# A new opening for an encoder kernel: quarters of x, first weights over two DMA queues, products by pairs of K blocks

## The chip, the cores and the metric

One Trainium2 chip, of which the program uses one core. The metric is the device time of one execution in microseconds (us); each version is run several times and the median is given.

## The reference

The kernel computes two layers of an encoder on 256 tokens of width 1024, all in float32. Each layer is a half-step feed-forward block, a mixer with two attention branches, and a second feed-forward block. The change touches the first feed-forward block of the first layer only:

```python
def rms_norm(x, g):
    y = x * lax.rsqrt(jnp.mean(x * x, axis=-1, keepdims=True) + EPS)
    return y * g

def swiglu(x, w_gate, w_up, w_down):
    return (jax.nn.silu(x @ w_gate) * (x @ w_up)) @ w_down

for l in range(2):
    x = x + 0.5 * swiglu(rms_norm(x, ffn1_norm[l]), ffn1_w_gate[l], ffn1_w_up[l], ffn1_w_down[l])
    ...   # neighbourhood attention and sliding-window attention, gated, into w_out
    x = x + 0.5 * swiglu(rms_norm(x, ffn2_norm[l]), ffn2_w_gate[l], ffn2_w_up[l], ffn2_w_down[l])
```

## The kernel before

The 256 tokens are two tiles of 128 (`t` is 0 or 1), and the width of 1024 is eight K blocks of 128. A float32 product is made of three products of rounded parts: every operand is split into a high part, made on ScalarE (ACT) by a copy, and a low part, the remainder, made on VectorE (DVE) by a subtraction. The high and low parts of x are the tiles `xh0, xl0` (tile 0) and `xh1, xl1` (tile 1); those of a piece of weights are `wh` and `wl`. Three matmuls then add x-high by w-high, x-high by w-low and x-low by w-high in PSUM. The helper `split_to` issues the two instructions of a split, `load` starts a weight transfer of 512 KB (two K blocks by 512 columns) into one of four buffers `raw` and splits it.

x stands with tokens on the partitions, so `norm` turns it on TensorE (PE): four transposes into a PSUM tile `tp`, a product with the gains (`gain`) into `xg`, and the split of `xg`. The factor of the norm itself (`rs_y`, one number for each token) is applied later, when the gate is taken. It comes from `square`: two sums of squares a tile on ACT, two small operations on DVE, a power on GpSimd (POOL).

The feed-forward block goes through its 2816 hidden columns in eleven chunks. A chunk has 256 gate and 256 up columns, which give one PSUM tile `g` of 512 columns for each token tile. The tiles `g` come from the pool `ps_g`, which has two buffers. When the 24 matmuls of a tile are done, ACT makes `sg` (the silu of the gate half) and DVE makes `hh` (times the up half); both read `g`, so its buffer is free only when `hh` is done, and the third `g` of the program goes into the buffer of the first.

`opening` replaces the first chunk's matmuls at the start of the program, where nothing is loaded yet. It interleaves the transfers, the norm without its factor, the first splits, warm-up matmuls on a blank tile (`warmup`), and the 48 products of chunk 0; it also issues the splits of the four weight pieces of chunk 1 (`second`) and the four squares.

The order on each engine comes from two places. The order on PE is that of the code. The order on DVE, ACT, POOL and of the DMA issues is made by a scheduler from a model of times when the program is built, except where the code chains instructions: `linked` ties each instruction of `opening` to the one before it on its engine, until `chain.clear()`.

Of the kernel before, what the change touches and what calls it, by code (L numbers as in the profile page):

```python
# [11 lines left out]
F32 = mybir.dt.float32  # L12
# [9 lines left out]
P = 128  # L22
# [34 lines left out]
def hybrid_encoder(ctx, tc, x, w_gu1, w_d1, w_in, b_gate, qk_gain, rpb, sink, t5,  # L57
# [20 lines left out]

    def fetch(t, h):
        if (t, h) == (0, 0):  # L80
            nc.sync.dma_start(wide[:, :HEAD + 512], x[:P, :HEAD + 512])
        else:
            nc.sync.dma_start(xs[t][:, h * 512:(h + 1) * 512],
                              x[t * P:(t + 1) * P, HEAD + h * 512:HEAD + (h + 1) * 512])

    fetch(0, 0)

# [7 lines left out]
    warmed = nc.scalar.activation(warm, ident[:, :1], AF.Silu)  # L95
# [92 lines left out]

    ssq = [None] * T

    def norm(t, n, half, apart=False):
        if half == 0:
            xT[t] = [act.tile([P, KD, P], F32R, name=f"x{p}{t}", tag=f"x{p}{t}") for p in "hl"]
            ssq[t] = small.tile([P, 2], F32, name="ssq", tag="ssq")
        ks = slice(4 * half, 4 * half + 4)
        tp = ps_tp.tile([P, 4, P], F32, name="tp", tag="tp")
        for i in range(4):
            k = 4 * half + i
            nc.tensor.transpose(tp[:, i, :], xs[t][:, k * P:(k + 1) * P], ident)
        xg = act.tile([P, 4, P], F32, name="xg", tag="xg", bufs=2)  # L200
        if apart and half == 1:
            for i in range(4):
                linked("act", lambda: nc.scalar.activation(xg[:, i, :], tp[:, i, :], AF.Copy,
                                                           scale=gain[:, n, 4 + i:5 + i]))
        else:
            linked("dve", lambda: nc.vector.tensor_tensor(
                xg, tp, gain[:, n, ks].unsqueeze(2).to_broadcast([P, 4, P]), ALU.mult))
        split_to(*(x[:, ks, :] for x in xT[t]), xg)
        if not apart:
            square(t, half)  # L210

    def square(t, half, junk=None):
        if junk is None:
            junk = act.tile([P, 512], BF16, name="junk", tag="xg", bufs=2)
        linked("act", lambda: nc.scalar.activation(junk, xs[t][:, half * 512:(half + 1) * 512], AF.Square,
                                                   accum_out=ssq[t][:, half:half + 1]))
        if half == 1:
            v = small.tile([P, 1], F32, name="ms", tag="ms")
            nc.vector.tensor_tensor(v, ssq[t][:, :1], ssq[t][:, 1:], ALU.add)
            nc.vector.tensor_scalar(v, v, 1.0 / D, EPS, op0=ALU.mult, op1=ALU.add)  # L220
            rstd[t] = rsqrt(v, 1)

    def opening(w, l):
        def piece(i, c=0):
            return load(w[l, 2 * i * P:(2 * i + 2) * P, c * 512:(c + 1) * 512].rearrange("(k p) n -> p k n", p=P),
                        2, 512)

        ps = [ps_g.tile([P, 512], F32, name="g", tag="g") for _ in range(T)]

        def steps(t, i):  # L230
            wh, wl = pieces[i]
            xh, xl = xT[t]
            for a, b in ((xh, wh), (xl, wh), (xh, wl)):
                for k in (2 * i, 2 * i + 1):
                    nc.tensor.matmul(ps[t], a[:, k, :], b[:, k % 2, :], start=a is xh and b is wh and k == 0,
                                     stop=b is wl and k == KD - 1)
            tick(2)

        pieces = []
        chain["act"] = warmed  # L240
        warmup(5)
        norm(0, 0, 0, True)
        pieces.append(piece(0))
        warmup(5)
# [17 lines left out]
        second += [piece(i, 1) for i in range(1, KD // 2)]  # L262
# [565 lines left out]
```

## Time and profile before

| | us |
|---|---|
| runs of the kernel | 1091.14, 1092.18, 1093.49 (median 1092.18) |
| the profiled execution | 1091.39 |
| its span, first to last instruction | 1089.6 |
| PE busy in the span | 1077.2 (99%) |
| DVE, ACT, POOL busy | 855.7 (79%), 658.7 (60%), 117.5 (11%) |
| read from memory | 210.59 MB, 194 GB/s over the span |

The views of the profile give times from the start of the span. A row of the timeline has the start, the length, the engine, the line of the code and the operation, what it writes and reads, and how many instructions were merged into the row; in brackets at its end stands how long the engine was idle before and what released it. PEld is the loading of the stationary operand, which runs beside the matmuls and shows waits more exactly than PE does; SPq is the queue that issues the transfers.

### The profile page before, as it was taken

Reading aid. Unit: us, or ns where it says so; the run is one execution under the profiler, and the core shown is the slowest. Engines: PE = TensorE matmul, PEld = TensorE weight load, DVE = VectorE, ACT = ScalarE, POOL = GpSimd, SP = SyncE. Lnnn points to the kernel's source line nnn. Section 1 sums busy time; section 2 is a strip of 40 time slices with the busy share of each in tenths; the row PEclk is TensorE's granted clock in tenths of the full one; section 3 lists DMA queues with packets and bytes.
Section 4 is the critical chain, followed back from the end, with each engine's and each line's share of the span. In section 5 each row is a group of like instructions: output and inputs, shape, how many; then the busy total and the mean of one; then the engine's idle time right before and its main releaser. Section 6 shows DMA issues by size and latency. Waiting matters only on the chain.

```text
span 1089.6 us, 14660 instructions
## 1 busy us (share of the span) xinstructions
PE 1077.2 (99%) x5137; PEld 889.5 (82%) x5137; DVE 855.7 (79%) x1298; ACT 658.7 (60%) x1002; POOL 117.5 (11%) x118
## 2 busy tenths in 40 slices
PE   9999999999999999999999999999999999999998
PEld 7888878888888888888878888888888888888887
DVE  6887787889886778778777787788888767878785
ACT  6665654788764556565465565457877646656552
POOL 1400000243520000000000000003534000000000
PEclk9999999999999999999999999999999999999999
DMA  8876565755654676666657766557666555776661
GB/s 241 267 222 216 189 197 171 234 189 152 189 179 135 201 224 212 210 197 203 193 172 219 228 204 211 162 164 236 183 190 178 178 166 166 225 235 198 212 188 71
DMA packets 98827, 212.63 MB, mean 195 GB/s; under 512 B 7568, under 2 KB 13744, under 8 KB 98752
## 3 DMA queue, kind: packets, MB, share of 16 engines
q1 hardware_dynamic: 98560, 211.60, 62.1%
q8 instruction: 40, 0.66, 0.2%
q0 software_dynamic: 192, 0.08, 0.1%
q14 instruction: 35, 0.29, 0.1%
HBM read 210.59 MB, written 1.06 MB: 194 GB/s over the span
## 4 chain that ended last, share of the span: by engine, by line
PE 86%; DVE 8%; ACT 3%; issue 2%; DMA 2%; ACTq 0%; DVEq 0%
PE g L168 19%; PE g L170 19%; PE g L169 19%; PE acc L168 5%; PE acc L170 5%; PE acc L169 5%; DVE wl L183 3%; PE tp L317 2%; ACT wh L182 1%; PE tp L168 1%; PE tp L169 1%; PE tp L170 1%; PE pt L572 1%; DMA raw<-in_w_d 1%; PE sc L551 1%
## 5 line engine op out<-in xcount | busy, mean ns | idle before, releaser
L183 DVE TENSOR_TENSOR wl<-raw,wh 128x1024 fp32r<-128x1024 f32 (+1 forms) x340 | 407.8, 1216 | 68.8 <-ACT wh L182 67.5
L182 ACT ACTIVATE wh<-raw 128x1024 fp32r<-128x1024 f32 (+1 forms) x340 | 348.9, 1046 | 111.9 <-PE g L170 35.0
L168 PE MATMUL g<-wh,xh 128*128 128x512 f32 (+1 forms) x976 | 389.9, 399 | 0.0
L170 PE MATMUL g<-wh,xl 128*128 128x512 f32 (+1 forms) x976 | 379.0, 388 | 0.7 <-DVE xl L183 0.7
L169 PE MATMUL g<-wl,xh 128*128 128x512 f32 (+1 forms) x976 | 377.6, 387 | 0.4 <-DVE wl L183 0.4
L170 PEld LDWEIGHTS g<-wh,xl 128*128 128x128 f32 x976 | 183.4, 188 | 41.4 <-DVE xl L183 2.1
L169 PEld LDWEIGHTS g<-wl,xh 128*128 128x128 f32 x976 | 184.1, 189 | 32.0 <-DVE wl L183 0.8
L168 PEld LDWEIGHTS g<-wh,xh 128*128 128x128 f32 x976 | 183.6, 188 | 30.9 <-DVE hh L449 0.2
L447 ACT ACTIVATE sg<-g,rs_y 128x256 f32<-128x256 f32 x88 | 41.4, 471 | 117.1 <-PE g L170 116.8
L347 DVE TENSOR_TENSOR u<-raw 128x512 f32<-128x512 f32 x56 | 38.7, 691 | 61.9 <-DMA raw<-in_w_d 61.3
L168 PE MATMUL acc<-wh,hi 128*128 128x512 f32 x200 | 79.3, 396 | 0.0
L170 PE MATMUL acc<-wh,lo 128*128 128x512 f32 x200 | 78.0, 390 | 0.0
L169 PE MATMUL acc<-wl,hi 128*128 128x512 f32 x200 | 77.9, 390 | 0.0
L174 POOL TENSOR_TENSOR rs_y<-ms,mhalf 128x1 f32<-128x1 f32 x12 | 6.7, 556 | 660.3 <-DVE ms L220 651.9
L449 DVE SCALAR_TENSOR_TENSOR hh<-g,rs_y,sg 128x256 f32<-128x256 f32 x88 | 42.2, 480 | 38.8 <-ACT sg L447 38.7
L182 ACT ACTIVATE corner<-raw 128x512 fp32r<-128x512 f32 x28 | 17.6, 630 | 54.7 <-DMA raw<-in_w_d 38.4
L564 POOL TENSOR_TENSOR S<-S,sm 128x512 f32<-128x512 f32 x32 | 37.2, 1161 | 71.4 <-DVE sm L563 45.2
L170 PEld LDWEIGHTS acc<-wh,lo 128*128 128x128 f32 x200 | 37.6, 188 | 8.1
L169 PEld LDWEIGHTS acc<-wl,hi 128*128 128x128 f32 x200 | 37.6, 188 | 7.4
L168 PEld LDWEIGHTS acc<-wh,hi 128*128 128x128 f32 x200 | 37.6, 188 | 7.4
L557 ACT ACTIVATE S<-S,mx 128x256 f32<-128x256 f32 x64 | 32.0, 501 | 7.4 <-DVE mx L554 7.4
L317 PEld LDWEIGHTS tp<-ident,hh 128*128 128x128 f32 x176 | 24.2, 140 | 14.1 <-DVE hh L449 3.4
(190 smaller groups left out, 1477.3 us busy)
## 6 DMA issues: line engine op xcount, KB each, us to landing
raw<-in_w_gu SPq DMA_DIRECT2D x176, 512.0 KB, 4.4
raw<-in_w_d SPq DMA_DIRECT2D x100, 512.0 KB, 4.3
raw<-in_w_in SPq DMA_DIRECT2D x64, 512.0 KB, 4.3
raw<-in_w_out SPq DMA_DIRECT2D x16, 512.0 KB, 3.6
bb<-in_b_gate SPq DMA_DIRECT2D x16, 256.0 KB, 3.5
raw<-in_w_bsw SPq DMA_DIRECT2D x8, 512.0 KB, 4.0
raw<-in_w_bna SPq DMA_DIRECT2D x8, 512.0 KB, 3.5
raw<-in_w_d SPq DMA_DIRECT2D x12, 256.0 KB, 2.6
```

Source lines behind the costliest of these rows:

```text
L168: nc.tensor.matmul(ps, xh, wh, start=first, stop=False)
L169: nc.tensor.matmul(ps, xh, wl, start=False, stop=False)
L170: nc.tensor.matmul(ps, xl, wh, start=False, stop=last)
L182: linked("act", lambda: nc.scalar.activation(hi, src, AF.Copy))
L183: linked("dve", lambda: nc.vector.tensor_tensor(lo, src, hi.bitcast(F32), ALU.subtract))
L317: nc.tensor.transpose(tp[:, SLOT[t][i], :], hh[:, i * P:(i + 1) * P], ident)
L347: sub = lambda to, x, y: nc.vector.tensor_tensor(to, x, y, ALU.subtract)
L447: nc.scalar.activation(sg, ps[:, :FC], AF.Silu, scale=rstd[t])
L449: nc.vector.scalar_tensor_tensor(hh, ps[:, FC:], rstd[t], sg, op0=ALU.mult, op1=ALU.mult)
L551: nc.tensor.matmul(ps[:, t, :], qT[:, h, t * P:(t + 1) * P], k[:, kidx(h), :], start=i == 0, stop=i == 1)
L557: nc.scalar.activation(S_[:, t, :], S_[:, t, :], AF.Exp, bias=mx[:, t:t + 1], scale=-1.0, accum_out=sm[:, t:t + 1])
L564: nc.gpsimd.tensor_tensor(S_, S_, sm.unsqueeze(2).to_broadcast([P, T, S]), ALU.mult)
```

## The change

- The x transfers are cut: the first half of each tile's width arrives as two quarters, and the first transfer is 192 KB (with the gains) in place of 320 KB.
- The first weight piece is issued by ACT, as two transfers of one K block (256 KB) each, beside SP's transfers; it was one of 512 KB on SP. The order on SP becomes: quarters of both tiles, the second piece, second halves of x, the rest.
- Turning, gain, split and products of the first half of x go by two K blocks at a time for both tiles; the first weight piece is split by one K block. The second half of x keeps its four K blocks.
- The four squares stay behind the last split of the opening in the code, as before.
- The loading of the silu table follows ACT's two transfers.

The core of the diff (`turned`, `gained`, `xpart`, `wpart` are the transposes, the gain and the two halves of a split for the K blocks named, each chained on its engine; `go` issues the products; the second letter of "hl" is the weights' part):

```diff
     def fetch(t, h):
         if (t, h) == (0, 0):
-            nc.sync.dma_start(wide[:, :HEAD + 512], x[:P, :HEAD + 512])
+            nc.sync.dma_start(wide[:, :HEAD + 256], x[:P, :HEAD + 256])
         else:
-            nc.sync.dma_start(xs[t][:, h * 512:(h + 1) * 512],
-                              x[t * P:(t + 1) * P, HEAD + h * 512:HEAD + (h + 1) * 512])
+            c0, c1 = (0, 256, 512, D)[h:h + 2]
+            nc.sync.dma_start(xs[t][:, c0:c1], x[t * P:(t + 1) * P, HEAD + c0:HEAD + c1])
...
+        def fetched(i, apart=None):
+            raws[i] = ring.tile([P, 2, 512], F32, name="raw", tag="raw", bufs=RAW)
+            for ks in (slice(0, 1), slice(1, 2)) if apart else (slice(0, 2),):
+                (apart or nc.sync).dma_start(raws[i][:, ks, :], source(i)[:, ks, :])
...
+        A, B, ALL = (0, 1), (2, 3), (0, 1, 2, 3)
+        fetched(0, nc.scalar)
         fetch(1, 0)
-        norm(1, 0, 0, True)
-        pieces.append(piece(1))
         fetch(0, 1)
         fetch(1, 1)
-        warmup(3)
-        steps(0, 0)
-        norm(0, 0, 1, True)
-        steps(1, 0)
-        pieces.append(piece(2))
-        norm(1, 0, 1, True)
-        pieces.append(piece(3))
+        chain["act"] = nc.scalar.activation(warm, ident[:, :1], AF.Silu)
+        fetched(1)
+        warmup(4)
+        turned(0, 0, A)
+        gained(0, 0, A, "dve")
...
+        go(0, (0,), "hh", "hl")
+        go(0, (1,), "hh")
+        go(0, (0, 1), "lh")
+        turned(0, 0, B)
+        gained(0, 0, B, "act")
+        go(1, (0, 1), "hh")
+        go(0, (1,), "hl")
+        go(1, (0, 1), "hl", "lh")
+        turned(1, 0, B)
+        fetch(0, 2)
+        fetch(1, 2)
+        fetched(2)
+        fetched(3)
+        gained(1, 0, B, "dve")
...
+        go(0, B, "hh", "lh")
+        go(1, B, "hh", "lh")
+        turned(0, 1, ALL)
+        turned(1, 1, ALL)
+        go(0, B, "hl")
+        go(1, B, "hl")
+        gained(0, 1, ALL, "act")
+        gained(1, 1, ALL, "dve")
+        xpart(0, 1, ALL, "h")
+        xpart(1, 1, ALL, "h")
+        wpart(2, (0, 1), "h")
...
         square(0, 0, idle)
         square(0, 1, idle)
-        second = [piece(0, 1)]
+        second = [load(source(0, 1), 2, 512)]
...
-        for i in (1, 2, 3):
+        for ks in ((4, 5), (6, 7)):
             for t in range(T):
-                steps(t, i)
+                go(t, ks, "hh", "lh", "hl")
```

The order on the engines changes in the first fifty or so instructions of DVE and ACT and is the same behind them. Two places are shown; a name's number tells one buffer of the program from another, and the line numbers are those of the version shown.

First, ACT in the opening. Before, from its first split to the last split of the four weight pieces of chunk 0 (`wh_130`, `wh_154`, `wh_189`, `wh_207`):

```order
L182 ACTIVATE xh0_116<-xg_124 128x512
L182 ACTIVATE wh_130<-raw_128 128x1024
L182 ACTIVATE xh1_140<-xg_148 128x512
L182 ACTIVATE wh_154<-raw_152 128x1024
L203 ACTIVATE xg_174<-tp_169,x0_82 128x128 x4
L182 ACTIVATE xh0_116<-xg_174 128x512
L182 ACTIVATE wh_189<-raw_187 128x1024
L203 ACTIVATE xg_198<-tp_193,x0_82 128x128 x4
L182 ACTIVATE xh1_140<-xg_198 128x512
L182 ACTIVATE wh_207<-raw_205 128x1024
```

Now, from the split of the second piece (`wh_123`) to that of the fourth; `tp_198` is the second half of tile 0 turned, `xg_205` that of tile 1 with its gain, made on DVE:

```order
L252 ACTIVATE wh_123<-raw_121 128x1024
L252 ACTIVATE xh1_145<-xg_144 128x256
L243 ACTIVATE xg_199<-tp_198,x0_82 128x128 x4
L252 ACTIVATE xh0_131<-xg_199 128x512
L252 ACTIVATE xh1_145<-xg_205 128x512
L252 ACTIVATE wh_177<-raw_175 128x1024
L252 ACTIVATE wh_181<-raw_179 128x1024
```

The splits of the third and fourth piece moved behind the gain and both splits of the second half of x; before, each tile's half was followed by one piece.

Second, the change from chunk 0 to chunk 1. Here ACT before, with the squares (L215), the splits of chunk 1's pieces (`wh_220` to `wh_245`) and the two `sg` of chunk 0:

```order
L215 ACTIVATE idle_104,ssq_118<-x0_82 128x512 x2
L182 ACTIVATE wh_220<-raw_218 128x1024
L215 ACTIVATE idle_104,ssq_142<-x1_83 128x512
L447 ACTIVATE sg_285<-g_109,rs_y_216 128x256
L215 ACTIVATE idle_104,ssq_142<-x1_83 128x512
L182 ACTIVATE wh_233<-raw_231 128x1024
L182 ACTIVATE wh_239<-raw_237 128x1024
L182 ACTIVATE wh_245<-raw_243 128x1024
L447 ACTIVATE sg_289<-g_110,rs_y_229 128x256
```

And ACT now, where chunk 1's pieces are `wh_236` to `wh_261` and tile 0's gate is `sg_289`:

```order
L207 ACTIVATE idle_103,ssq_110<-x0_82 128x512 x2
L181 ACTIVATE wh_236<-raw_234 128x1024
L207 ACTIVATE idle_103,ssq_111<-x1_83 128x512 x2
L181 ACTIVATE wh_249<-raw_247 128x1024
L181 ACTIVATE wh_255<-raw_253 128x1024
L181 ACTIVATE wh_261<-raw_259 128x1024
L523 ACTIVATE sg_289<-g_108,rs_y_232 128x256
L181 ACTIVATE wh_369<-raw_367 128x1024
L523 ACTIVATE sg_293<-g_109,rs_y_245 128x256
```

Tile 0's `sg` moved from behind the first piece of chunk 1 and three squares to behind all four pieces and all four squares.

DVE at the same place before:

```order
L219 TENSOR_TENSOR ms_213<-ssq_118 128x1
L220 TENSOR_SCALAR ms_213<-ms_213 128x1
L183 TENSOR_TENSOR wl_221<-raw_218,wh_220 128x1024
L449 SCALAR_TENSOR_TENSOR hh_287<-g_109,rs_y_216,sg_285 128x256
L219 TENSOR_TENSOR ms_226<-ssq_142 128x1
L220 TENSOR_SCALAR ms_226<-ms_226 128x1
L183 TENSOR_TENSOR wl_234<-raw_231,wh_233 128x1024
L183 TENSOR_TENSOR wl_240<-raw_237,wh_239 128x1024
L107 SCALAR_TENSOR_TENSOR qkg_96<-qkg_96 128x2 x2
L183 TENSOR_TENSOR wl_246<-raw_243,wh_245 128x1024
L449 SCALAR_TENSOR_TENSOR hh_291<-g_110,rs_y_229,sg_289 128x256
```

And DVE now; `qkg` are two small products that need a transfer issued by POOL after the last square's `rs_y`:

```order
L182 TENSOR_TENSOR wl_237<-raw_234,wh_236 128x1024
L211 TENSOR_TENSOR ms_242<-ssq_111 128x1
L212 TENSOR_SCALAR ms_242<-ms_242 128x1
L182 TENSOR_TENSOR wl_250<-raw_247,wh_249 128x1024
L182 TENSOR_TENSOR wl_256<-raw_253,wh_255 128x1024
L106 SCALAR_TENSOR_TENSOR qkg_95<-qkg_95 128x2 x2
L182 TENSOR_TENSOR wl_262<-raw_259,wh_261 128x1024
L525 SCALAR_TENSOR_TENSOR hh_291<-g_108,rs_y_232,sg_289 128x256
L182 TENSOR_TENSOR wl_370<-raw_367,wh_369 128x1024
```

Tile 0's `hh` moved from behind the first low part of chunk 1 (`wl_221`) to behind the fourth (`wl_262`) and behind `qkg`.

PE at this place now, with the waits; `g_297` is the first tile of chunk 1, the third of the pool of two, and PE's order from here on is the same as before:

```order
L271 MATMUL g_109<-wh_181,xh1_145 128x512 x2
L271 MATMUL g_109<-wh_181,xl1_146 128x512 x2
L271 MATMUL g_109<-wl_182,xh1_145 128x512 x2
L167 MATMUL g_297<-wh_236,xh0_131 128x512 [waits DVE_49]
L168 MATMUL g_297<-wl_237,xh0_131 128x512
L169 MATMUL g_297<-wh_236,xl0_132 128x512
```

The count of DVE operations for which `g_297` waits is the one that `hh_291` reaches; before, its counterpart `g_293` waited in the same way for `hh_287`.

More of the change, by code (lines that the diff above doesn't have):

```diff
@@ L189, in hybrid_encoder, with norm @@
     ssq = [None] * T
-    def norm(t, n, half, apart=False):
+    def norm(t, n, half):
         if half == 0:
@@ L200, in norm @@
         xg = act.tile([P, 4, P], F32, name="xg", tag="xg", bufs=2)
[L201 to L207, printed above, removed]
+        nc.vector.tensor_tensor(xg, tp, gain[:, n, ks].unsqueeze(2).to_broadcast([P, 4, P]), ALU.mult)
         split_to(*(x[:, ks, :] for x in xT[t]), xg)
-        if not apart:
-            square(t, half)
+        square(t, half)
     def square(t, half, junk=None):
@@ L223, in opening, with source @@
     def opening(w, l):
-        def piece(i, c=0):
-            return load(w[l, 2 * i * P:(2 * i + 2) * P, c * 512:(c + 1) * 512].rearrange("(k p) n -> p k n", p=P),
-                        2, 512)
+        def source(i, c=0):
+            return w[l, 2 * i * P:(2 * i + 2) * P, c * 512:(c + 1) * 512].rearrange("(k p) n -> p k n", p=P)
         ps = [ps_g.tile([P, 512], F32, name="g", tag="g") for _ in range(T)]
[L230 to L237, printed above, removed]
@@ new lines, in turned @@
+        def turned(t, half, ks):
+            if (t, half) not in tps:
+                tps[t, half] = ps_tp.tile([P, 4, P], F32, name="tp", tag="tp")
+                xgs[t, half] = act.tile([P, 4, P], F32, name="xg", tag="xg", bufs=2)
+                if half == 0:
+                    xT[t] = [act.tile([P, KD, P], F32R, name=f"x{p}{t}", tag=f"x{p}{t}") for p in "hl"]
+            for i in ks:
+                k = 4 * half + i
+                nc.tensor.transpose(tps[t, half][:, i, :], xs[t][:, k * P:(k + 1) * P], ident)
```

65 lines of the change are left out of this document (57 added, 8 removed).

## The prediction

> **What bounds the kernel now.** I read the page first, then busy time by stretches, then the timeline of the first 27 us, where everything that the change touches lies.
>
> ```profile
> PE 1077.2 (99%) x5137; PEld 889.5 (82%) x5137; DVE 855.7 (79%) x1298; ACT 658.7 (60%) x1002; POOL 117.5 (11%) x118
> ```
>
> ```profile
> core 0: us, PE busy (x) PEld busy (x) DVE busy (x) ACT busy (x) POOL busy (x), PEclk, DMA share, GB/s
> 7.40:20.30 12.90, 12.74 (x58) 9.58 (x56) 9.60 (x12) 10.76 (x25) 0.55 (x1) 1.00 0.84 273
> 20.30:26.40 6.10, 5.68 (x25) 4.38 (x25) 5.28 (x9) 4.25 (x6) 3.43 (x6) 1.00 0.83 198
> 26.40:1089.60 1063.20, 1053.05 (x5038) 871.11 (x5036) 838.59 (x1271) 640.59 (x969) 112.80 (x105) 1.00 0.62 194
> ```
>
> The second fence is a table of stretches with the busy time of each engine. PE is busy 99% of the span, and from 26.4 us to the end 1053.05 of 1063.2 us. What the opening gains or loses therefore reaches the end almost whole: behind it PE has no slack in which a shift could vanish, and the orders behind it are unchanged. So the question is when PE gets through the opening and into chunk 1. The waits of the weight loads from 5 us on, by who ended them (in all, times, longest):
>
> ```profile
> PEld pt L572 <- issue: 4.9, 4, 1.2
> ...
> PEld g L169 <- DVE wl L183: 0.8, 1, 0.8
> ...
> PEld g L168 <- DVE hh L449: 0.2, 1, 0.2
> ```
>
> The timeline gives the prices:
>
> ```profile
> 0.73 1.28 ACT L95 ACT_TABLE_LOAD   x1 [0.73 <-PEq L817]
> 1.66 2.50 PE L118 MATMUL idle<-blank 128*128 128x512 f32 x5 [1.66 <-DVE blank L113]
> 3.74 0.88 PEld L199 LDWEIGHTS tp<-ident,x 128*128 128x128 f32 x4 [0.30 <-issue]
> 5.05 0.69 DVE L206 TENSOR_TENSOR xg<-tp,x 128x512 f32<-128x512 f32 x1 [3.37 <-PE tp L199]
> 6.30 0.42 PEld L199 LDWEIGHTS tp<-ident,x 128*128 128x128 f32 x4 [0.23 <-DMA x<-in_x]
> 6.71 0.95 PE L118 MATMUL idle<-blank 128*128 128x512 f32 x3
> 7.40 1.23 DVE L183 TENSOR_TENSOR wl<-raw,wh 128x1024 fp32r<-128x1024 f32 x1 [0.26 <-ACT wh L182]
> 7.42 0.30 PEld L235 LDWEIGHTS g<-wh,xh 128*128 128x128 f32 x2 [0.20 <-ACT wh L182]
> 8.54 0.68 DVE L206 TENSOR_TENSOR xg<-tp,x 128x512 f32<-128x512 f32 x1
> 10.74 1.13 ACT L203 ACTIVATE xg<-tp,x 128x128 f32<-128x128 f32 x4
> 11.90 0.63 ACT L182 ACTIVATE xh<-xg 128x512 fp32r<-128x512 f32 x1
> 12.44 1.05 ACT L182 ACTIVATE wh<-raw 128x1024 fp32r<-128x1024 f32 x1
> 14.23 0.42 PEld L235 LDWEIGHTS g<-wl,xh 128*128 128x128 f32 x2
> 14.69 0.41 PEld L235 LDWEIGHTS g<-wh,xh 128*128 128x128 f32 x2
> 16.04 0.58 ACT L215 ACTIVATE idle<-x 128x512 f32<-128x512 f32 x1
> 16.78 0.60 ACT L215 ACTIVATE idle<-x 128x512 f32<-128x512 f32 x1
> ```
>
> PE gets its first product at 7.42. A matmul of 512 columns costs 0.23 us (pairs at 14.23 and 14.69), at the slow rate of the first warm-ups about 0.43 (five last 2.50 with the tail of the last; three last 0.95 later). A transpose costs 0.11 (four loads in 0.42 at 6.30), slow 0.22 (0.88 at 3.74); its output reached DVE 0.43 after the last slow load (4.62 to 5.05). ACT steps on by 1.16 after four gains of 128 columns (10.74 to 11.90), 0.54 after a split of 512 (11.90 to 12.44) and 0.74 after a square (16.04 to 16.78). DVE's low part of 1024 takes 1.23 and steps 1.14 (7.40 to 8.54); of 512, 0.69. And the change to chunk 1:
>
> ```profile
> 19.26 0.48 ACT L447 ACTIVATE sg<-g,rs_y 128x256 f32<-128x256 f32 x1 [0.19 <-PE g L235]
> 19.77 0.48 DVE L449 SCALAR_TENSOR_TENSOR hh<-g,rs_y,sg 128x256 f32<-128x256 f32 x1
> 20.15 0.19 ACT L215 ACTIVATION_READ_ACCUMULATOR idle<-x 128x1 f32 x1
> 20.24 2.95 ACT L182 ACTIVATE wh<-raw 128x1024 fp32r<-128x1024 f32 x3
> 20.30 0.19 PEld L168 LDWEIGHTS g<-wh,xh 128*128 128x128 f32 x1 [0.21 <-DVE hh L449]
> 22.61 0.19 PEld L169 LDWEIGHTS g<-wl,xh 128*128 128x128 f32 x1 [0.84 <-DVE wl L183]
> 23.80 0.23 DVE L107 SCALAR_TENSOR_TENSOR qkg<-qkg 128x2 f32<-128x2 f32 x2
> 23.95 1.22 DVE L183 TENSOR_TENSOR wl<-raw,wh 128x1024 fp32r<-128x1024 f32 x1
> 26.37 0.58 PEld L317 LDWEIGHTS tp<-ident,hh 128*128 128x128 f32 x4
> ```
>
> This fence decides the case. Three ACT splits of 1024 in a row last 2.95, so one steps 0.95. At 20.30 PE's first load of chunk 1 is released by `hh` of DVE, which ended at 19.77 + 0.48 = 20.25: with two buffers for `g`, chunk 1 can't begin before tile 0's `hh` of chunk 0. That costs only 0.21 now, because `sg` and `hh` run as soon as tile 0 is done. Behind it PE loses 0.84 once more at 22.61 to a late low part; 0.04 of that is the usual gap between loads, so 0.80.
>
> **The change, part by part.** *Transfers.* How fast the first bytes come:
>
> ```profile
> 0.74 0.38 SPq L81 DMA_DIRECT2D x<-in_x  x1
> 1.18 0.42 SPq L140 DMA_DIRECT2D raw<-in_w_gu  x1
> 2.63 0.94 SPq L83 DMA_DIRECT2D x<-in_x  x2
> x<-in_x SPq DMA_DIRECT2D x3, 256.0 KB, 6.3
> x<-in_x SPq DMA_DIRECT2D x1, 320.0 KB, 2.9
> ```
>
> The first 320 KB, issued at 0.74, had landed 2.9 later, at 3.64. Behind them went 512 KB of weights, then 256 KB of x, which released PE at 6.30: 768 KB in 2.66. Now x's first quarter (192 KB) is issued beside ACT's first half piece (256 KB). In the table of stretches above the 16 engines are busy 0.84 of the time at 273 GB/s with one queue, so I let the two queues share that rate: both land with 448 KB, at 3.64 + 128 x 2.66/768 = 4.1, and tile 1's quarter with 832 KB, at 5.4. Ends: if the queues don't slow each other, tile 1's quarter lands with SP's own 320 KB at 3.6; with 256 KB more ahead of it, at 6.3.
>
> The Trainium skill ("DMA: Bandwidth & Descriptors", section "Issuing engines are not separate DMA queues") speaks against a gain from the second queue: the transfers of all issuing engines run on the same 16 DMA engines and interleave, and only the time to issue them is saved. By that rule the sum is the 4.7 below; with independent queues the first product would wait for its splits alone, come at 5.7 instead of 6.3, and the sum would be 4.1. No row here shows two queues at work.
>
> ACT's two issues (0.38 to 0.47 each, as SP's rows) delay the silu table (1.28) from 0.73 to about 1.7, and ACT is ready at about 3.2: hidden by the landing at 4.1, at most 0.9 if not. On SP tile 1's second half now waits until ACT's first half piece has landed (a semaphore used again), and the third and fourth piece queue behind it: issued at about 4.2 instead of 3.1, while transfers ahead of them are still moving; hidden, at most 1.1 on the third piece, needed at 14.7.
>
> *First product.* PE now turns tile 1's quarter (two transposes) and runs two warm-ups ahead of its first product: 5.4 + 0.22 to 0.44 + 0.46 to 0.86 gives 6.1 to 6.7. The splits for it are not later: half piece split at 4.1 + 0.63; gain (DVE, 256 columns, between 0.69 for 512 and nothing, on the line through 0.69 and 1.23 about 0.42) and ACT's split (about 0.42 likewise) end at 5.7. I take 6.3, nearer the low end, since the warm-ups after 5.4 are likely at the fast rate; 1.1 earlier than now. At the slow rate throughout, the first pair's products would add up to 12 x 0.2 = 2.4.
>
> *First pair and second pair of K blocks.* Twelve products and four transposes: 12 x 0.23 + 4 x 0.11 = 3.2, so 9.5; with 0.2 until the last transpose stands in PSUM, DVE makes tile 1's gain of the second pair at 9.7, then tile 0's low part: 0.34 + 0.42, so 10.45. This wait is new, since tile 1's transposes stand behind all products of the first pair. PE then does six products (1.4) and four transposes (0.44 + 0.2): ACT begins the gain of tile 0's second half at 12.5.
>
> *Third and fourth piece.* ACT does the four gains (1.16) and both tiles' splits of 512 (2 x 0.54) before the third piece: 14.74. It ends at 15.8, where it ended at 12.44 + 1.05 = 13.5 before. PE, done with the second pair at about 13.8, stands for 2 us, then has 24 products (5.5) and 0.3 for the low part: done at 21.6, against 20.3 before. The early start has been spent.
>
> *Into chunk 1.* In ACT's order tile 0's `sg` stands behind the third and fourth piece (2 x 0.95), four squares (4 x 0.74) and three splits of chunk 1 (3 x 0.95) before the fourth: 14.74 + 1.9 + 2.96 + 2.85 = 22.45, which ends at 23.5. On DVE `hh` stands behind the fourth low part, and that behind `qkg`: before, the last square ended at 20.15 + 0.19 = 20.34 and `qkg` came 3.46 later at 23.80 (norm factor, then a transfer issued by POOL). Now the last square ends at 14.74 + 1.9 + 2.96 + 0.95 = 20.55, so `qkg` comes at 24.0, the low part at 24.15, `hh` at 24.15 + 1.14 = 25.3 and ends at 25.8. The fourth piece's transfer waits for the fourth low part of chunk 0 (ended at 18.2) and is hidden if it lands by 22.5; a slower landing adds what it is late.
>
> PE's first matmul of chunk 1 so starts at 25.8, not 20.30: 5.5 later, of which PE idles 4.2. All splits of chunk 1 are then ready, so the 0.80 at 22.61 goes. Tile 1's gate is ready at about 27.4 and needed at 31.3: hidden.
>
> *Sum:* 25.8 - 20.3 - 0.8 = 4.7 slower. The profiled execution took 1091.39, 1.8 over its span: 1096.1. The median of the runs is 0.8 above it; I name 1096.5, half of that added. A measurement of this kernel can tell some 0.2% (2.2 us) from no change, so this would show.
>
> **The rivals.** *The clock falls in the pause* (chance 0.20). PE would idle 4.2 us at one place, longer than anywhere in the trace (longest wait of a load 1.2). The slow rate at the start lasted from 1.66 to between 4.2 and 6.7, where warm-ups step 0.43 and later ones 0.23; if the pause brings it back for some 3.6 us, eight matmuls cost 0.43 instead of 0.23: 1.7 more, 1098.2. For it: the rate did begin slow after rest. Against it: no row here shows a fall. The Trainium skill ("TensorE: Matmul & The Clock Gate", section "Why this matters for your kernels") says that a gap over about 3 us can return the clock to half; by that rule 1098.2 is the result, if the pause covers the monitor's window, which runs free.
>
> *The opening goes through sooner* (0.14). If DVE and ACT hand over faster around the second pair, the gain of the second half starts at 11.0 instead of 12.5. Squares and `qkg`'s chain move along, and `hh` ends 1.5 sooner, at 24.3: 3.2 slower, 1095.0. For it: the quarters' operations are sized by a line, not by rows.
>
> *The pause doesn't come* (0.07), the case of the other side. If ACT never waited from 4.1 on, it would need 2 x 0.54 for half pieces, 4 x 0.33 for quarters' splits, 2 x 0.25 + 1.16 for gains, 2 x 0.54, seven splits of 1024 at 0.95 and 2.96 for squares: 14.8, so 18.9 at the end of chunk 1's last split instead of 23.5. The last square then ends at 16.0, `qkg` comes at 19.5, the low part at 19.6, and `hh` ends at 21.2: 21.3 - 20.3 - 0.8 = 0.2 slower, 1092.0, no difference that can be told. The place is ACT between 6 and 14.7; with `hh` ended by 23.3 the kernel is not slower by 0.2%. Against it: ACT's gain of the second half needs transposes that PE does only after products which themselves need DVE and ACT.
>
> *The early start counts and the rest stays* would be 1.1 + 0.8 faster, 1089.9; it needs `hh` before `wl_250`, and the order has it behind `wl_262` (0.01).
>
> **How the numbers follow.** The 0.4 for the median's distance is in each of the times. Forecast (PE enters chunk 1 between 24.8 and 27.0: 1095.5 to 1097.7) 0.58; clock 0.20; sooner 0.14; no pause 0.07; early start alone 0.01. The range reaches from 1094.2, an opening 2.3 sooner than mine, to 1099.0, the clock's fall with PE entering at 26.6; what lies outside is the case without a pause and the tails. Slower by over 0.2%: 0.58 + 0.20 + nearly all of 0.14, 0.90; within 0.2%: most of 0.07 and the rest of 0.14, 0.08; faster 0.02.
>
> **What would show it.** Right: first product near 6.3; ACT's third piece split near 14.7; in PE's waits one on `hh` of about 4 us, and the first load of chunk 1 at 25 to 27; no wait on a low part behind it; from there the same distances as before. Clock: matmuls 0.43 apart behind the pause. Wrong: chunk 1 begun before 23.3, or PE catching up later, which would mean that PE had slack behind the opening that I did not see.

## The result: 7 us slower

| | changed | before |
|---|---|---|
| median (lowest to highest) | 1099.44 us (1098.96 to 1100.84, 4 runs) | 1092.36 us (1091.14 to 1093.49, 4 runs) |
| ratio | 1.0071, 95% interval 1.0059 to 1.0083 | |
| profiled execution, its span | 1099.8, 1098.0 | 1091.39, 1089.6 |

A second set of runs of the changed kernel (`r_after`, below) gave 1100.39 us, ratio 1.0080 (1.0067 to 1.0094). The kernel is slower, as forecast, but by more: 1096.5 was named, with 1099.0 as the upper end.

The page of the changed kernel and PE's waits in it (weight loads; in all, times, longest):

```profile
PE 1079.8 (98%) x5132; PEld 891.0 (81%) x5132; DVE 856.0 (78%) x1303; ACT 657.5 (60%) x1003; POOL 109.9 (10%) x118
```

```profile
PEld g L167 <- DVE hh L525: 3.7, 1, 3.7
PEld tp L393 <- DVE hh L525: 3.6, 6, 1.1
PEld g L271 <- ACT wh L252: 2.9, 2, 2.4
```

The busy shares hardly moved (PE 99% before, 98% now). The waits did: PE has two new pauses, 2.4 us for the third piece's split and 3.7 us for `hh`, where the kernel before waited 0.2. The waits of 3.6 in the middle lie at the ends of later stages and were there before (3.4).

The timeline of the changed kernel, the rows that answer to those of the prediction:

```profile
6.63 0.33 PEld L271 LDWEIGHTS g<-wh,xh 128*128 128x128 f32 x1
10.89 0.42 DVE L248 TENSOR_TENSOR xg<-tp,x 128x256 f32<-128x256 f32 x1 [3.09 <-PE tp L237]
13.83 1.14 ACT L243 ACTIVATE xg<-tp,x 128x128 f32<-128x128 f32 x4 [2.07 <-PE tp L237]
16.06 1.99 ACT L252 ACTIVATE wh<-raw 128x1024 fp32r<-128x1024 f32 x2
17.15 0.30 PEld L271 LDWEIGHTS g<-wh,xh 128*128 128x128 f32 x2 [2.43 <-ACT wh L252]
21.55 0.19 ACT L207 ACTIVATION_READ_ACCUMULATOR idle<-x 128x1 f32 x1
22.70 0.79 POOL L102 DMA_DIRECT2D qkg<-in_qk_gain  x1
24.17 1.06 ACT L181 ACTIVATE wh<-raw 128x1024 fp32r<-128x1024 f32 x1 [0.54 <-DMA raw<-in_w_gu]
26.16 0.23 DVE L106 SCALAR_TENSOR_TENSOR qkg<-qkg 128x2 f32<-128x2 f32 x2 [1.08 <-DMA qkg<-in_qk_gain]
27.44 0.48 DVE L525 SCALAR_TENSOR_TENSOR hh<-g,rs_y,sg 128x256 f32<-128x256 f32 x1
27.97 0.19 PEld L167 LDWEIGHTS g<-wh,xh 128*128 128x128 f32 x1 [3.65 <-DVE hh L525]
34.95 0.59 PEld L393 LDWEIGHTS tp<-ident,hh 128*128 128x128 f32 x4
```

PE has its first product at 6.63, 0.8 earlier than before, waits 2.43 at 17.15, and enters chunk 1 at 27.97 instead of 20.30. And the stretches behind the two pauses (busy time of PE, PEld, DVE, ACT, POOL; then the granted clock, the share of the DMA engines, GB/s):

```profile
14.78:18.19 3.41, 1.41 (x6) 0.67 (x4) 2.53 (x4) 3.38 (x6) 0.00 (x0) 1.00 0.42 145
18.19:21.60 3.41, 3.36 (x9) 2.51 (x9) 2.77 (x5) 3.35 (x9) 0.55 (x1) 0.50 0.56 171
...
25.02:28.43 3.41, 0.45 (x2) 0.41 (x3) 2.33 (x6) 1.98 (x4) 0.60 (x2) 1.00 0.87 186
28.43:31.84 3.41, 3.41 (x10) 2.63 (x9) 2.59 (x4) 1.06 (x1) 1.37 (x3) 0.50 0.99 328
31.84:1095.00 1063.16, 1055.92 (x5051) 873.49 (x5050) 836.88 (x1268) 638.03 (x968) 103.86 (x103) 1.00 0.62 193
```

After each pause PE runs at half its clock (the 0.50 in the rows) for 3.41 us. The first slow stretch is covered by the second pause, in which PE waits for `hh` in any case. In the second, eight matmuls stand 0.43 apart instead of 0.23: 1.6 us.

The account against the profile before: 27.97 - 20.30 = 7.67 at the entry, less the 0.80 at 22.61 that is gone, plus 1.6 of slow clock, 8.5. The first transposes of `hh` come at 34.95 instead of 26.37, 8.6 later; the last weight load of the program comes 8.1 later (1093.46 against 1085.37), and the times differ by 8.4. The medians differ by 7.1 and, in the second set, by 8.8.

### The profile page after: what moved, and what is told of

Its sections match the earlier page's. It is cut to its first block, busy times and chain, and to the rows that moved or that the text cites. A ratio compares the mean times of both kernels' runs of the same rounds, so it can differ in the third digit from the quotient of the medians.

```text
span 1098.0 us, 14661 instructions
## 1 busy us (share of the span) xinstructions
PE 1079.8 (98%) x5132; PEld 891.0 (81%) x5132; DVE 856.0 (78%) x1303; ACT 657.5 (60%) x1003; POOL 109.9 (10%) x118
## 4 chain that ended last, share of the span: by engine, by line
PE 85%; DVE 8%; ACT 3%; issue 2%; DMA 2%; POOL 0%; DVEq 0%; ACTq 0%
PE g L167 19%; PE g L169 19%; PE g L168 19%; PE acc L167 5%; PE acc L169 5%; PE acc L168 5%; DVE wl L182 3%; PE tp L393 2%; ACT wh L181 1%; PE tp L167 1%; PE tp L169 1%; PE tp L168 1%; DMA raw<-in_w_d 1%; PE pt L648 1%; PE sc L627 1%
## 5 line engine op out<-in xcount | busy, mean ns | idle before, releaser
L182 DVE TENSOR_TENSOR wl<-raw,wh 128x1024 fp32r<-128x1024 f32 (+1 forms) x336 | 402.5, 1215 | 66.6 <-ACT wh L181 65.3
L181 ACT ACTIVATE wh<-raw 128x1024 fp32r<-128x1024 f32 (+1 forms) x336 | 344.2, 1044 | 110.4 <-PE g L169 36.0
```

The costliest lines, as they stand in the source:

```text
L181: linked("act", lambda: nc.scalar.activation(hi, src, AF.Copy))
L182: linked("dve", lambda: nc.vector.tensor_tensor(lo, src, hi.bitcast(F32), ALU.subtract))
```

## The experiments

The theory after reading the profile: in the orders of ACT and DVE tile 0's `sg` and `hh` stand behind the squares and chunk 1's splits, and those begin late, so `hh` comes at 27.9; PE can't pass it, since `g` has two banks; the pause then slows the clock. Rivals: the splits and transfers of chunk 1 are late themselves; the clock costs nothing, or doesn't come from the pause; PE has slack behind the opening. The kernel before was run beside each set on the same chip; across sets, only the ratios compare.

| kernel | median us | before | ratio (95% interval) |
|---|---|---|---|
| e1_gate_first | 1095.91 | 1091.75 | 1.0036 (1.0024 to 1.0048) |
| e2_third_bank | 1095.86 | 1091.75 | 1.0034 (1.0021 to 1.0047) |
| e3_warm | 1100.03 | 1091.75 | 1.0076 (1.0063 to 1.0088) |
| e4_constants_late | 1098.33 | 1091.75 | 1.0059 (1.0047 to 1.0071) |
| r_after | 1100.39 | 1091.63 | 1.0080 (1.0067 to 1.0094) |
| e3_warm_again | 1100.69 | 1091.63 | 1.0085 (1.0071 to 1.0099) |
| e5_piece_ahead | 1098.94 | 1091.63 | 1.0069 (1.0057 to 1.0082) |
| e6_all | 1091.07 | 1091.63 | 0.9993 (0.9984 to 1.0002) |
| e7_hold20 | 1096.25 | 1092.06 | 1.0040 (1.0028 to 1.0053) |
| e8_hold80 | 1102.08 | 1092.06 | 1.0094 (1.0080 to 1.0108) |
| e9_one_queue | 1092.63 | 1092.06 | 1.0003 (0.9994 to 1.0013) |
| e10_before_bank | 1092.15 | 1092.06 | 1.0001 (0.9992 to 1.0010) |
| e11_warm48 | 1101.81 | 1091.46 | 1.0083 (1.0069 to 1.0098) |
| e12_hold10 | 1093.38 | 1091.46 | 1.0016 (1.0007 to 1.0025) |
| e13_hold40 | 1095.95 | 1091.46 | 1.0038 (1.0025 to 1.0050) |

**The wait on `hh`: a third bank, or `hh` placed earlier.** In e2 the first sum of chunk 1 goes elsewhere:

```diff
+                    third = ps_acc.tile([P, 512], F32, name="g", tag="pt") if n == 0 and (c, t) == (1, 0) else None
-                    ps = both[t] if first else project(t, pieces, 512)
+                    ps = both[t] if first else project(t, pieces, 512, third)
```

> Tile 0's sum of chunk 1 gets a bank of its own, so that PE needn't wait for hh_291 before it begins chunk 1; the orders of ACT and DVE stay up to there. Theory (the wait on hh is what costs: PE stood 3.65 us for it at 27.97): PE goes on at about 24.4, when its chunk 0 is done, perhaps with waits on single pieces of chunk 1 (second to fourth split start 20.2 to 24.2), no pause over 1 us, no fall of the clock behind it, so 3.6 + 1.6 less than the changed kernel: 1094.3 us, from 1093.5 to 1096. Rival (the pieces of chunk 1 are late themselves, so that the wait only changes its name): within 1 us of the changed kernel's 1099.4.

In e1 the second to fourth piece of chunk 1 are loaded behind tile 0's gate, chained to it, and the constants (with `qkg`) go behind `hh` as well:

```diff
-        second += [load(source(i, 1), 2, 512) for i in range(1, KD // 2)]
...
+        rest = lambda: [load(source(i, 1), 2, 512) for i in range(1, KD // 2)]
...
-        defer(24, "constants", constants)
+        defer(48, "constants", constants)
...
+                    if first and t == 0:
+                        chain.update(act=gate, dve=both_done)
+                        second += more()
+                        chain.clear()
```

> sg and hh of tile 0 stand ahead of the second to fourth split of chunk 1 in ACT's and DVE's orders, and the constants with qkg behind them. Theory (the place of sg and hh in the orders is what costs): the first load of chunk 1 is released by hh at about 24.5 to 25 instead of 27.97, and the splits come later, each 0.5 to 1 us, with PE working through eight K blocks at 0.7 us each beside them; about 5 us less than the changed kernel: 1094.3, from 1093.5 to 1096.5. Rival (ACT's and DVE's work is the bound, wherever hh stands: the same wait then falls on the low parts wl): within 1 us of 1099.4.

Both came out near 1095.9, inside the expected ranges at their upper ends and 4 to 5 us below the changed kernel by the ratios. PE's waits up to 60 us, of e2 and then e1:

```profile
PEld g L271 <- ACT wh L252: 2.9, 2, 2.4
PEld g L168 <- DVE wl L182: 1.2, 3, 0.5
PEld tp L393 <- DVE hh L526: 1.0, 2, 0.5
```

```profile
PEld g L271 <- ACT wh L252: 2.9, 2, 2.4
...
PEld g L168 <- DVE wl L182: 0.4, 2, 0.2
...
PEld g L167 <- DVE hh L525: 0.2, 1, 0.2
```

In both the pause of 3.7 is gone and the small waits that come in its place don't fill it; the pause of 2.4 stays. So the pieces were not late: the place of `hh`, with two banks, was what PE paid for. It is shown by two different edits: e2 keeps the orders up to `hh` and adds a bank, e1 keeps the two banks and moves `hh` ahead of three pieces and of `qkg`. In its profile e2 lost part of what it had won far behind the opening, in one wait near 759 us that the profile of the kernel before doesn't have:

```profile
PEld tp L572 <- issue: 1.6, 1, 1.6
```

**`qkg` ahead of `hh`.** One number puts the constants behind `hh`:

```diff
-        defer(24, "constants", constants)
+        defer(48, "constants", constants)
```

> The changed kernel with the constants (four transfers issued by POOL, and the qkg operation on DVE, which waited 1.08 us for its transfer at 26.16) issued behind hh. Theory (qkg stands in DVE's order ahead of the last low part and of hh, and its transfer lands late): hh_291 ends 1.0 sooner, near 26.9, and PE enters chunk 1 at 27.0: 1098.4, from 1097.9 to 1098.9. Rival (the fourth piece's transfer and its split, at 24.17, set hh, not qkg): 1099.4, within 0.4. A further gain up to 1.6 is possible where the shorter pause spares the clock window.

Measured 1098.33; by the ratios 1.3 us below the first set of the changed kernel and 2.3 below the second, with intervals that overlap. The trace is clearer: `hh` started at 25.42; in the second profile of the changed kernel, whose clock rose at nearly the same time (5.78, here 5.56), it started at 26.44: 1.0, as expected.

**The third piece ahead of the gains.** The edit also holds `sg` and `hh` in their places (not shown).

```diff
+        wpart(2, (0, 1), "h")
+        wpart(2, (0, 1), "l")
         gained(0, 1, ALL, "act")
         gained(1, 1, ALL, "dve")
...
-        wpart(2, (0, 1), "h")
```

> The third piece's split on ACT and its low part on DVE are moved ahead of the gains of the second half, into the 2.1 us in which ACT waits there; the order from the first square on stays. Theory (ACT's chain through this place sets the last square, qkg and hh): the fourth piece's split, the squares and hh come 0.95 earlier, the first pause shrinks from 2.4 to about 0.9, the second stays: 0.95 less than the changed kernel beside it, from 0.4 to 1.5 with the clock's windows. Rival (DVE's or a transfer's part of the chain decides): no change, within 0.3.

1098.94, 1.45 below `r_after`, so inside the range (the intervals overlap), but not all by the path expected. The rows of e5:

```profile
19.61 0.19 ACT L207 ACTIVATION_READ_ACCUMULATOR idle<-x 128x1 f32 x1
24.64 0.23 DVE L106 SCALAR_TENSOR_TENSOR qkg<-qkg 128x2 f32<-128x2 f32 x2 [1.50 <-DMA qkg<-in_qk_gain]
26.46 0.29 PEld L167 LDWEIGHTS g<-wh,xh 128*128 128x128 f32 x1 [6.14 <-DVE hh L530]
```

The last square came 0.84 earlier than in `r_after` (19.61 against 20.45) and the first pause shrank, yet PE entered chunk 1 only 0.52 earlier (26.46 against 26.98): `qkg`'s transfer, issued 0.85 earlier, took 3.9 us instead of 3.5, and PE now stood 6.14 for `hh`. An earlier opening alone helps little while `hh` stands behind `qkg`.

**The clock.** e3 keeps PE busy on zeros in both pauses, 8 and 20 matmuls into a bank that nothing reads, and holds `sg` and `hh` in their places; e3_warm_again is the same kernel; e11 has 40 short matmuls (`keep[:, :P]` from `ident_r` and `ident_r`) in place of the last line's 20.

```diff
+        warmup(8, keep)
         for ks in ((4, 5), (6, 7)):
             for t in range(T):
                 go(t, ks, "hh", "lh", "hl")
+        warmup(20, keep)
```

> The changed kernel with 28 matmuls on zeros into a bank that nothing reads, 8 in the first pause (before K blocks 4 and 5) and 20 in the second (before chunk 1); sg and hh are held where they stood. Theory (hh sets PE's entry, and the slow clock behind the pauses costs on top of it): hh ends within 0.3 us of 27.92, the clock stays full, matmuls behind the entry step 0.22 instead of 0.43, and 1.6 us are gained: 1097.8, from 1097.2 to 1098.4. Rival (the slow matmuls are hidden by later waits for pieces, so the clock is only seen and not paid): 1099.4, within 0.5. Second rival (the clock does not come from the pause): the matmuls behind the entry stay 0.43 apart and the time is 1099.4 or more.

> The changed kernel once more, beside the next three on one chip: 1099.4 as before, from 1098.9 to 1100.0, with a mean granted clock of 0.996 to 0.998. In single executions the first product should come between 6.0 and 6.7, by where the slow clock of the start ends (5.5 to 8.3 in the runs so far).

> The kernel with 28 matmuls on zeros once more, beside the changed kernel on the same chip; the first time it kept the clock full (1.000 against 0.996) and yet its median was 1100.0. Theory (the slow windows cost 1.6 us behind the second pause): 1.6 less than the changed kernel beside it, 1097.8. Rival (what PE gains there it loses again later, in its waits on hh at the ends of the stages, which were 5.3 us in all against 3.6): within 0.6 of the changed kernel beside it.

> e3_warm with 40 matmuls of ident_r (128 columns) instead of 20 of zeros (512 columns) in the second pause: the same 4.5 us of work for PE, 20 more instructions. Rule (a lead that PE has behind the opening is lost in its later waits on hh): again 1100 to 1100.7, waits on hh of 5 us or more behind 50 us. Scatter (these waits differ from kernel to kernel whatever the lead): the waits on hh go to some other sum between 3 and 7 us and the time with them; with 3.5 us the 1.6 show, 1098. Both: clock 0.999 or 1.000.

In their profiles the clock stayed full from its first rise on (the row is e3_warm_again behind the place of the second pause), and no time was gained: 1100.03, 1100.69 and 1101.81, where the first theory said 1097.8.

```profile
26.26:33.09 6.83, 6.21 (x30) 5.03 (x30) 4.36 (x7) 1.33 (x2) 2.98 (x10) 1.00 0.82 257
```

The pause as the cause of the slow clock is shown; its price at the end of the program is not. The four executions of `r_after` say no more: the profiled one, with a mean clock of 0.995, took 1100.17, the three with 0.997 took 1099.88 to 1100.89. In `r_after` the clock was at half for two stretches behind the second pause, 14 matmuls; e3_warm_again entered chunk 1 at the same time (27.03 against 26.98) and was 2.75 ahead at 33 us. It was 0.1 ahead at the end. Where the lead went stands in PE's waits behind 50 us, of `r_after` and of e3_warm_again:

```profile
PEld tp L393 <- DVE hh L525: 3.3, 5, 0.8
```

```profile
PEld tp L397 <- DVE hh L533: 6.3, 6, 1.5
```

Their first at the end of a stage, the same load in both:

```profile
147.96 0.20 PEld L393 LDWEIGHTS tp<-ident,hh 128*128 128x128 f32 x2 [0.53 <-DVE hh L525]
```

```profile
146.25 0.20 PEld L397 LDWEIGHTS tp<-ident,hh 128*128 128x128 f32 x2 [1.55 <-DVE hh L533]
```

e11 met neither of its expectations: its waits on `hh` behind 50 us were 3.8, yet it wasn't faster. In the profiled execution its clock rose only at 10.23, and PE entered chunk 1 at 29.71. Its five executions lie apart, 1099.51 twice and 1101.81 to 1102.63; the profiled one is among the long ones.

**Has PE slack behind the opening?** The kernel before, with 10, 20, 40 and 80 idle matmuls ahead of chunk 2:

```diff
+    def hold(n):
+        keep = ps_acc.tile([P, 512], F32, name="keep", tag="pt")
+        for _ in range(n):
+            nc.tensor.matmul(keep[:, :P], ident_r, ident_r, start=True, stop=True)
...
+                if n == 0 and c == 2:
+                    hold(20)
```

> The kernel before with 20 matmuls of ident_r on itself (128 columns, into a bank that nothing reads) ahead of chunk 2: PE alone is held up there for a known time, some 2.2 us by 0.11 for a transpose of that size, at about 37 us; the profile gives it exactly. Theory (behind the opening PE has no slack, so that what is lost there reaches the end): the time rises by what the 20 take, 2.2 us, from 1.6 to 2.6: 1093.8. Rival (PE's later waits on hh at the ends of the stages give back or take what PE is ahead or behind, so that a shift fades): clearly less than half of it, under 1 us.

> The same with 80 such matmuls, some 8.8 us. Theory (no slack): 8.8 more than the kernel before, or what the profile shows that they take, within 0.7: 1100.4. Rival (a shift fades): under 6.

> The kernel before with 10 matmuls of ident_r ahead of chunk 2, 1.16 us (0.1155 each in the run with 20). One to one: 1.2 more than the kernel before, 1093.3, within 0.6. Scatter: 0 to 3.5 more, with the waits on hh behind 50 us differing from the 3.4 of the kernel before by as much as the time differs from 1.2.

> The same with 40, 4.6 us. One to one: 4.6 more than the kernel before, 1096.7, within 0.6. Scatter: 3.5 to 7 more, with the waits on hh differing as much. If both holds lie on a line of slope 1 from an offset of about 1 to 2 us, what costs is the insertion itself (orders of ACT and DVE that changed in two places with it).

| matmuls | they took | median, more than before (95% interval) | profiled execution, more than before (1091.39) | its waits on `hh` behind 50 us |
|---|---|---|---|---|
| 10 | 1.19 | 1.9 (0.8 to 2.7) | 2.6 | 5.2 |
| 20 | 2.31 | 4.2 (3.1 to 5.8) | 6.2 | 7.2 |
| 40 | 4.54 | 4.5 (2.7 to 5.5) | 3.9 | 3.4 |
| 80 | 9.01 | 10.0 (8.7 to 11.8) | 9.4 | 4.3 |

The profile of the kernel before has 3.4 us of these waits. Their rows for 20 and 40:

```profile
PEld tp L322 <- DVE hh L456: 7.2, 7, 1.7
```

```profile
PEld tp L322 <- DVE hh L456: 3.4, 6, 0.8
```

PE has no slack by what can be measured: no interval lies below what the matmuls took, and between stage ends the distance to the kernel before stays the same to 0.1 (2.91 at 67 us and 2.89 at 100 us with 20 matmuls). But at the ends of the stages `hh` makes PE wait between 0.2 and 1.9 us, and the sum differs from profile to profile by up to 4 us, in no order of the holds. Each sum is that of one execution: two profiles of one kernel gave 3.6 and 3.3, two of e3 5.3 and 6.3, and the profiled execution with 20 was the longest of its five, that with 40 the shortest.

That a shift fades at the stage ends falls with the 40 and the 80, and with e6 below, whose lead of 1.8 at 67 us was still 1.5 at the end; the one-to-one line falls with the 20, whose interval lies above 2.31. Two more places scatter. A wait of 1.4 to 1.6 us like that of e2 stands in the profiles of e9, e10 and e11, and not in that of the kernel before. And with 20 matmuls `qkg`'s transfer took 3.3 us where it took 2.3 to 2.5 in the kernel before and with 10, 40 and 80; a low part of chunk 1 came late behind it, and the first transposes of `hh` stood at 27.09 instead of 26.37: 0.7 of the 2.91 arose ahead of the hold.

So an edit at the opening carries a scatter of 0 to 2 us in the median that isn't its own (0.7, 1.9, 0 and 1.0 in the four rows). What decides it stays open, and with it the clock's price.

**One version from all of it, and its parts.** e6 has the third bank, the late constants, the second half's transposes placed earlier on PE, and the third piece between the two tiles' splits (shown for ACT, alike on DVE):

```diff
+        turned(0, 1, ALL)
...
+        turned(1, 1, ALL)
         go(1, B, "hh", "lh")
-        turned(0, 1, ALL)
-        turned(1, 1, ALL)
...
         xpart(0, 1, ALL, "h")
-        xpart(1, 1, ALL, "h")
         wpart(2, (0, 1), "h")
+        xpart(1, 1, ALL, "h")
```

> A version from the readings so far: tile 0's sum of chunk 1 in a bank of its own; the constants behind chunk 1; tile 0's transposes of the second half right behind tile 1's of the first, tile 1's ahead of its products; on ACT the third piece's split between tile 0's and tile 1's. Theory: both pauses go, PE is done with chunk 0 at about 19.2 and goes on into chunk 1 with no wait over 0.5; the first transposes of hh start near 24.9, where the kernel before has them at 26.4: 1.5 less than the kernel before, 1090.2, from 1089 to 1091.5. Rival (the transfers of the pieces or DVE's low parts take the place of the pauses): 1091.7 to 1094, no faster than before.

e10 gives the kernel before e2's edit and the late constants, and nothing else; e9 is e6 with all opening transfers in one queue:

```diff
-        fetched(0, nc.scalar)
+        fetched(0, nc.sync)
```

> The kernel before with two of the three remedies that stand in e6_all and none of the changed opening: tile 0's sum of chunk 1 in a bank of its own, the constants behind chunk 1. Theory (the gain of e6_all comes from the early start): PE's waits of 0.2 at 20.30 and 0.8 at 22.61 shrink a little, 0 to 0.6 less than the kernel before, 1091.3, and e6_all stays faster in its trace by 1 or more at the first transposes of hh. Rival (e6_all's gain comes from these two alone): as fast as e6_all or faster, 1090.5 to 1091.

> e6_all with the first piece's two halves issued by SP behind x's first quarter, not by ACT: all opening transfers in one queue. Theory (the 16 engines are shared, so the second queue saves no more than the time of issue): tile 1's quarter and what follows are issued 0.9 later and land up to 0.9 later, the halves land within 0.3 of where they did, the silu table is loaded 0.9 earlier; the first product comes 0.2 to 0.9 later, and the time is 0.2 to 0.9 longer than e6_all's. Rival (the second queue brings its own rate): the halves land 1 or more later, and the time is 1 to 2 longer. Second rival (the slow clock of the start hides it all): no difference that can be told from e6_all.

The rows of e6, and below them those of e9:

```profile
1.19 1.37 SPq L84 DMA_DIRECT2D x<-in_x  x3
5.15 0.38 PEld L237 LDWEIGHTS tp<-ident,x 128*128 128x128 f32 x2 [0.27 <-DMA x<-in_x]
18.87 0.19 PEld L167 LDWEIGHTS g<-wh,xh 128*128 128x128 f32 x1
24.32 0.58 PEld L393 LDWEIGHTS tp<-ident,hh 128*128 128x128 f32 x4
```

```profile
2.12 1.38 SPq L84 DMA_DIRECT2D x<-in_x  x3
6.36 0.29 PEld L237 LDWEIGHTS tp<-ident,x 128*128 128x128 f32 x2 [2.07 <-DMA x<-in_x]
```

In e6 both pauses are gone and PE enters chunk 1 at 18.87, 1.4 earlier than in the kernel before; the first transposes of `hh` come 2.0 earlier. The time is 9.3 us below the changed kernel on the same chip and 0.6 below the kernel before, which the interval doesn't tell from none: the forecast of 1.5 was not reached in the median. e10 gained nothing, and its first transposes of `hh` stand at 26.33, 0.04 earlier than before, so what e6 has over the kernel before in its trace comes from the new opening. In e9 tile 1's quarter was issued 0.93 later (the first of the three in its row, at 2.12 instead of 1.19) and released PE 1.21 later. Its ratio is 0.0010 above e6's, within the two intervals: the expected 0.2 to 0.9 us can be neither confirmed nor ruled out. The rest of e9's trace doesn't help, since its clock rose at 9.60 and that of e6 at 5.34. No version here is faster than the kernel before by what can be measured.

## Why the forecast was right in direction and too small

What held: the mechanism. The early start was spent by the first pause; PE came to `hh` and stood there; the 0.80 at 22.61 went; the distance at the entry reached the end to about half a us in the profiles (8.6 and 8.1 in the first). e1 and e2 show that it was `hh`'s place. That PE stood 3.65 us, near the 4.2 forecast, is in part luck: it was done with chunk 0 at 24.32, not at 21.6, and `hh` was late by nearly as much. That the case without a pause (1092.0) didn't come is seen in the 2.07 us which ACT waited for the transposes, the reason given against it.

What failed is the size of one term and the place of another. The entry into chunk 1, 25.8 in the sum, came at 27.97 and 26.98 in the two profiles of the changed kernel, and the slow clock behind the pause (1.6 and 2.8 us there) stood at nothing in the sum. Step by step:

- *ACT's gain of the second half at 12.5.* In the profile it came at 13.83, and so the last square ended at 21.74, not 20.55: 1.2 of the miss. This is one execution's: there the half clock of the start lasted to 7.95, which the prediction priced for the first pair (up to 2.4) and left out of the sum. In `r_after`, with the clock full from 5.78, the gain came at 12.74 and the last square ended at 20.64, within 0.25 and 0.1 of the forecast. But that execution paid 2.8 instead of 1.6 behind the pause, and the times were alike.
- *`qkg` 3.46 after the last square.* It was 4.42, 1.0 of the miss, and 4.52 in `r_after`. The reading of the row at 23.80 was right: in the kernel before the transfer, issued at 21.31, landed 2.5 later, and `qkg` began at once. (DVE had been busy until 23.69, and a gap of 0.11 gets no bracket.) What failed is the carrying over. In the changed kernel the time from the last square to the issue was the same to 0.01, but the transfer took 3.4 us, 3.5 in `r_after`. The fourth piece's transfer, which was to be hidden if it landed by 22.5, held its split until 24.17 (0.54 of idle ACT); it was hidden only because `qkg` came later still.
- *The clock, put among the rivals at 0.20.* It should have been in the forecast: the pause that I named at 4.2 us was longer than the 3.41 of a window, and the clock fell behind it in both profiles of the changed kernel and in e4 and e5, by 1.6 as that rival had it (8 matmuls) or more. The rule of the Trainium skill ("TensorE: Matmul & The Clock Gate", section "Why this matters for your kernels"), a gap over about 3 us, had it so, and the trace agrees for this pause; for the first one it differs, since 2.43 us were enough there, and the measurement decides. Its 1.6 us stand in the account of the profile; what they cost in the median is open, as told.

The view of `qkg`'s transfer and the stretch from its issue to its landing, in the kernel before and then in the changed kernel:

```profile
DMA to landing us min/median/max: 2.5/2.5/2.5
...
21.31:23.77 2.46, 2.04 (x9) 1.36 (x8) 2.36 (x2) 2.46 (x4) 2.46 (x6) 1.00 0.69 213
```

```profile
DMA to landing us min/median/max: 3.4/3.4/3.4
...
22.70:26.13 3.43, 2.04 (x9) 1.32 (x8) 2.36 (x2) 2.89 (x4) 2.92 (x6) 1.00 0.82 223
```

The DMA engines were busier in the second stretch, 0.82 against 0.69 (0.88 in `r_after`). That this made the transfer longer is likely but not tested: it took 3.3 once with the old opening, with 20 matmuls, at a share of 0.71.

The two entry terms (1.2 and 1.0) and the clock (1.6) make 3.8: with 4.7 they are the 8.5 of the account. For `r_after` the entry is 1.2 late, nearly all of it `qkg`, and the clock 2.8: 8.7, where its first transposes of `hh` came 8.8 later than before (35.20).

The sharing of the transfers held: in e6, whose transfers are those of the changed kernel, tile 1's quarter released PE at 5.15, where the prediction had 5.4, and in e9, with one queue and both halves ahead of it, at 6.36, near the 6.3 given as the end. Of these 1.21 us 0.93 are the later issue; from issue to release it took 4.24 instead of 3.96. The rule of the Trainium skill ("DMA: Bandwidth & Descriptors", section "Issuing engines are not separate DMA queues") is that a second issuing engine saves only the time of issue; the trace agrees but for the 0.28 that are left.

## What to carry to other kernels

Follow a moved block to the buffer that the next stage waits for: the early start was worth 0.8 us at the first product and the place of `hh` behind it cost 4 to 5, and either a third bank or a few places earlier in the order gave that back. A transfer's time read in one trace is not a constant: the same 4 KB took 2.5 us before and 3.4 to 3.9 in the profiles of the changed kernel and of e4 and e5. And before a change of a microsecond is credited, look at the waits that scatter elsewhere: here the sum of six or seven of them moved by up to 4 us from profile to profile.

## What the hardware showed

The clock is decided in windows of 3.41 us that don't start with the program. In the first profile of the changed kernel it changed at 7.95, 18.19, 21.60, 28.43 and 31.84, each a whole number of 3.41 behind the one before; the first rise fell at 5.3 to 10.2 us in these profiles. And the same pause of 2.43 us, from about 13.5 to 16, slowed the next window or did not, by where the windows lay. `r_after` and then e4, the window with the pause and the one behind it:

```profile
12.61:16.02 3.41, 1.45 (x9) 0.93 (x7) 1.99 (x3) 3.25 (x8) 0.00 (x0) 1.00 0.54 171
16.02:19.43 3.41, 3.37 (x8) 2.70 (x9) 2.76 (x5) 3.38 (x7) 0.55 (x1) 0.50 0.29 77
```

```profile
12.38:15.80 3.42, 1.54 (x10) 1.02 (x8) 1.99 (x3) 3.18 (x8) 0.00 (x0) 1.00 0.51 161
15.80:19.21 3.41, 3.22 (x13) 2.37 (x14) 2.68 (x5) 3.38 (x8) 0.55 (x1) 1.00 0.30 52
```

PE busy for 1.45 us of a window (1.35 in e1, 1.41 in the first profile) was followed by half clock, 1.54 (1.56 in e2) by full clock. Once at half, a window with 2.69 us of work (`r_after`, from 26.26) was followed by another slow one. So a pause well under 3.41 us is enough, and a pause shown in one execution may bring a slow window in it and none in the next.
